# A hybrid attention and state space layer on one core: gate units and the mean square after attention, moved from GpSimd to VectorE

## The chip, the cores and the metric

The kernel runs on one core of one Trainium2 chip. A core has TensorE (PE, matmuls), VectorE (DVE), ScalarE (ACT), GpSimd (POOL) and a queue that only issues transfers (SP); ACT and POOL issue transfers too. Each engine works off its own list of instructions in a fixed order. The metric is device microseconds of one execution, as the median over some runs.

## The reference, cut to what matters

The layer is decoder-like, 1024 positions plus 16 meta tokens, 1024 channels, all in float32:

```python
xn = rmsnorm(h, norm_mix)
q, k, v, u, g_att, g_ssm = jnp.split(xn @ w_in, offs, axis=-1)
attn = sliding_window_attention(q, k, v, sinks)
y = s5_ssm(u, ...)                      # a linear recurrence over the positions
z = jax.nn.gelu(y)
za, zb = jnp.split(z @ w_glu, 2, axis=-1)
ssm = za * jax.nn.sigmoid(zb)
merged = (jax.nn.sigmoid(g_att) * rmsnorm(attn, attn_branch_norm)
          + jax.nn.sigmoid(g_ssm) * rmsnorm(ssm, ssm_branch_norm))
h = h + merged @ w_out                  # then a SwiGLU block
```

What the change touches is the part between attention and `z`: the two gates, the mean square of `attn` that its norm needs, and the product gate x norm x `attn`.

## The kernel before, in words

Activations are held with channels on the 128 partitions and positions along the free side. Each float32 product is made of three passes over a rounded part and a remainder of both operands, so each loaded weight tile `raw` is cast on ACT to `wh` (line 103) and its remainder `wl` is a subtraction (line 104), on POOL unless the caller names another engine. The passes are the matmuls of line 122.

A gate unit (`g_unit`, line 540) is one of 32: unit numbers 0 to 15 make the state space gate (`which` = 1, written to `sg_d`), 16 to 31 the attention gate (`which` = 0). A unit is 8 x 3 matmuls of 128x512, a sigmoid on ACT into a tile `sg` (two buffers), and for `which` = 0 also: a load of attention's output from DRAM into `a` (line 553), its product with the broadcast root `rs_at` (line 554, POOL), a product with the norm's gain and `sg` (line 555, DVE), and a transfer to `pa_d` issued by ACT (line 557). Every second unit loads and splits one weight tile. Units 0 to 6 are put into the attention loop.

After attention the program text has this order. `W`, the state of the recurrence over 130 chunks, is loaded (line 765, 4160 KB). Then attention's output is read back in eight tiles `atf` of 128x1024 (two buffers), squared on ACT and added up in `acc` by seven additions (line 777, POOL). `rstd_cols` makes `rs_at` of it: 8 small matmuls (line 748), a copy of the sum to `ms_at` (line 751, DVE), thirteen tiny instructions on DVE for the reciprocal root (`rsqrt`, lines 151 to 159), matmuls that broadcast it (line 757) and two copies (line 759). Then comes the scan over `W` on DVE: 31 iterations of four instructions that depend on each other (lines 784 to 788), then eight blocks of two `step`s (lines 207 to 213). Then gate units 7 to 31, and then the eight blocks `y` (lines 819, 821: two chains of small matmuls, a Gelu into `z`, transposes `zT`), whose loads `uty`, `tp`, `ct` have three buffers. After them come the products with `w_glu` (`za`, `zb`), with weights split on POOL again.

This order is not the order of execution: a planner sorts the instructions into the engines' lists. It goes by a cost model of its own, takes the instruction whose operands are ready by that model, and among several of them the one that stands first in the text. On the chip the lists are then fixed: an engine whose next instruction waits does nothing else, however much of its list is ready.

Of the kernel before, what the change touches and what calls it, by code (L numbers as in the profile page):

```python
# [8 lines left out]
F32 = mybir.dt.float32  # L9
# [4 lines left out]
ALU = mybir.AluOpType  # L14
# [3 lines left out]
P = 128  # L18
# [16 lines left out]
CK, CV, CU, CGA, CGS = 1024, 1280, 1536, 2560, 3584  # L35
# [11 lines left out]
def hybrid_layer_kernel(ctx: ExitStack, tc: tile.TileContext, x, meta_tokens, norm_mix, w_in, q_norm, k_norm,  # L47
                        attn_sinks, lam_re, lam_im, log_dt, ssm_b_re, ssm_b_im, ssm_c_re, ssm_c_im, ssm_d,
                        w_glu, attn_branch_norm, ssm_branch_norm, w_out, norm_ffn, w_ffn_in, w_ffn_out, out):
    nc = tc.nc  # L50
    x, out = x[0], out[0]
    w_in, w_glu, w_out, w_ffn_in, w_ffn_out = w_in[0], w_glu[0], w_out[0], w_ffn_in[0], w_ffn_out[0]

    def sbuf(name, bufs, side="left"):
        return tc.tile_pool(name=name, bufs=bufs, side=side, reuse_waits="tile")
# [41 lines left out]
    def w_tile(src, shape, name, lo=None, pool=pool_r):  # L97

        raw = pool.tile([P, 1024], F32, tag="raw", name=f"raw_{name}")
        nc.sync.dma_start(out=raw.rearrange("p (a b) -> p a b", a=shape[0]), in_=src)  # L100
        hi = pool_w.tile([P, 1024], F32R, tag="w", name=f"wh_{name}")
        lw = pool_w.tile([P, 1024], F32R, tag="w", name=f"wl_{name}")
        nc.scalar.copy(hi, raw)  # L103
        (lo or nc.gpsimd).tensor_tensor(out=lw, in0=raw, in1=hi.bitcast(F32), op=ALU.subtract)  # L104
        return tuple(t.rearrange("p (a b) -> p a b", a=shape[0]) for t in (hi, lw))

    def w_cols(w, c0, n, name, lo=None, pools=(pool_r,)):

        per = 1024 // n
        parts = []  # L110
        for i in range(KB // per):
            src = w[i * per * P:(i + 1) * per * P, c0:c0 + n].rearrange("(a p) n -> p a n", p=P)
            parts.append(w_tile(src, (per, n), f"{name}_{i}", lo, pools[i % len(pools)]))
        return lambda kb, part: parts[kb // per][part][:, kb % per, :]
# [299 lines left out]
    with sbuf("pp", 1) as pp:  # L414
# [47 lines left out]
        for blk in range(8):  # L462
# [36 lines left out]
            for e in range(2):  # L499
                for j in range(2):  # L500
                    o = bank(f"v{blk}{e}{j}", "q" if j else "x")
                    for k in range(2):
                        g = e + 4 * j + 2 * k
# [26 lines left out]
    def cols_unit(w, h, name):  # L530

        o = bank(name)
        off = OFF[h]
        mm3(o, w, lambda kb, part: cur[h][part][:, kb, off:off + 512], KB)
        return o

    cur, OFF = xn, (16, 0)
    g_w = {}

    def g_unit(i, pool, bufs):  # L540

        which, f, h = 1 - i // 16, i // 2 % 8, i % 2
        if h == 0:
            g_w[which, f] = w_cols(w_in, (CGA, CGS)[which] + f * P, P, f"g{which}{f}")
        cols = slice(512 * h, 512 * h + 512)
        o = cols_unit(g_w[which, f], h, f"g{which}_{f}{h}")
        sg = pool.tile([P, 512], F32, tag="sg", bufs=bufs, name=f"sg{which}{f}{h}")
        nc.scalar.activation(out=sg, in_=o, func=AF.Sigmoid)
        if which:
            nc.scalar.dma_start(out=sg_d[f][:, cols], in_=sg)  # L550
            return
        a_ = pool.tile([P, 512], F32, tag="a", name=f"a{f}{h}")
        nc.sync.dma_start(out=a_, in_=at_d[f][:, cols])
        nc.gpsimd.tensor_tensor(out=a_, in0=a_, in1=rs_at[:, cols], op=ALU.mult)
        nc.vector.scalar_tensor_tensor(out=a_, in0=a_, scalar=gates[:, 0, f:f + 1], in1=sg,
                                       op0=ALU.mult, op1=ALU.mult)
        nc.scalar.dma_start(out=pa_d[f][:, cols], in_=a_)

    with sbuf("ag", 1, "right") as ag, sbuf("at", 2) as at:
# [170 lines left out]
        ng = NPRE  # L730
        for i in range(ng):
            g_unit(i, ag, 1)
        stages = ((q_proj, 10), (values, 0), (p_turn, 1), (scores, 4), (q_turn, 6))
        for i in range(-10, 32):
            for f, ahead in stages:
                if 0 <= i + ahead < 32:
                    f(i + ahead)
            if i in GAT:
                g_unit(ng, ag, 1)
                ng += 1  # L740
    kvp_cm.__exit__(None, None, None)

    def rstd_cols(acc, nb, name, pool):


        o = bank(f"ssq_{name}", "x")
        for b in range(nb):
            nc.tensor.matmul(o[:, b:b + 1], acc[:, b * P:(b + 1) * P], ones[:, 0:1].bitcast(F32),
                             start=True, stop=True)
        ms = pool.tile([P, nb], F32, tag=f"ms{nb}", name=f"ms_{name}")  # L750
        nc.vector.tensor_copy(ms, o[:, 0:nb])
        r = rsqrt(ms, P, nb, pool, name)
        rs = pool.tile([P, nb * P], F32, tag=f"rsb{nb}", name=f"rsb_{name}")
        for h in range(0, nb, 4):
            o = bank(f"rsb_{name}{h}", "x")
            for b in range(4):
                nc.tensor.matmul(o[:, b * P:(b + 1) * P], r[:, h + b:h + b + 1].to_broadcast([P, P]), ident,
                                 start=True, stop=True)
            nc.scalar.copy(rs[:, h * P:(h + 4) * P], o)
        return rs  # L760
# [3 lines left out]
    W = sp.tile([P, 2, GRP // 2, NCH], F32, name="W")  # L764
    nc.sync.dma_start(out=W, in_=v_d)
    gp = scan.enter_context(sbuf("gp", 2))
    with sbuf("vp", 2) as vp:

        acc = vp.tile([P, D], F32, tag="acc", bufs=1, name="acc_at")
        for f in range(KB):  # L770
            a_ = vp.tile([P, D], F32, tag="atf", name=f"atf{f}")
            nc.sync.dma_start(out=a_, in_=at_d[f])
            if f == 0:
                nc.scalar.activation(out=acc, in_=a_, func=AF.Square)
            else:
                nc.scalar.activation(out=a_, in_=a_, func=AF.Square)
                nc.gpsimd.tensor_tensor(out=acc, in0=acc, in1=a_, op=ALU.add)
        rs_at = rstd_cols(acc, 8, "at", sp)


# [1 line left out]
    for c in range(5, NCH - 1, 4):  # L782
        s1 = W[:, :, :, c]
        nc.vector.tensor_tensor(out=m, in0=W[:, :, :, c - 4].unsqueeze(1).to_broadcast([P, 2, 2, GRP // 2]),
                                in1=a32.rearrange("p (k r) g -> p k r g", k=2), op=ALU.mult)
# [7 lines left out]

    yp_cm = sbuf("yp", 2)
    yp = yp_cm.__enter__()
    for i in range(ng, 32):
        g_unit(i, gp, 2)


    zt = new_a("zt")  # L800
    for blk in range(8):
# [13 lines left out]
        for hh in range(2):  # L815
            o = bank(f"y{blk}{hh}")
            for k in range(4):
                g = 4 * hh + k
# [5 lines left out]
                out=z[:, :, 64 * hh:64 * hh + 64].rearrange("p t (g c) -> p g t c", c=16),  # L824
# [20 lines left out]
    with sbuf("mp", 2) as mp:  # L845
        ssm, acc = {}, {}
# [75 lines left out]
    with sbuf("op", 2) as op_:  # L922
# [37 lines left out]
        for n in range(2):  # L960
            w = w_cols(w_out, n * 512, 512, f"o{n}", nc.vector)
            cols = slice(512 * n, 512 * n + 512)
# [331 lines left out]
```

## Time and profile before

| | |
|---|---|
| median of 3 runs | 1725.21 us (1721.61 to 1725.79) |
| the profiled execution | 1730.69 us, its span 1728.9 us |
| PE busy | 1594.5 us, 92% of the span |
| DVE busy | 1200.3 us, 69% |
| ACT busy | 696.6 us, 40% |
| POOL busy | 438.4 us, 25% |
| mean granted clock of PE | 0.962 of full speed |

PE is the busiest engine by far, so a microsecond counts where PE stands still or runs at a lower clock. All times in the rows below are microseconds from the start of the span; attention ends at about 549, the first `za` product starts at about 765.

### The profile page before, as it was taken

What the parts mean: (1) busy time and instruction counts of PE and PEld (TensorE: products, weight loads), DVE (VectorE), ACT (ScalarE), POOL (GpSimd) and SP (SyncE); (2) the same over time, 40 slices, a digit from 0 to 9 for tenths busy, and PEclk for the clock granted to TensorE, in tenths of its full rate; (3) what the DMA queues carried; (4) which work ended last, traced back from release to release, by engine and by line L of the source; (5) the groups of instructions that cost most, each with busy time, mean ns of one, the idle gap of its engine ahead of it and who ended that gap; (6) DMA issues with size and microseconds to landing.
All of it is one profiled execution on the core that took longest, in us unless ns stands there. A gap on an engine that the chain in (4) does not pass through costs nothing.

```text
span 1728.9 us, 22182 instructions
## 1 busy us (share of the span) xinstructions
PE 1594.5 (92%) x8002; PEld 1326.6 (77%) x8002; DVE 1200.3 (69%) x2245; ACT 696.6 (40%) x1363; POOL 438.4 (25%) x312
## 2 busy tenths in 40 slices
PE   7999978989989959699998898899999999899999
PEld 5788868778867848588887786688888888678887
DVE  7779886999983899351115668966665666299973
ACT  4424335878974311262222232533333333234330
POOL 0001103334332613402332400111111112256441
PEclk9999989999989979899999899899999999999999
DMA  5264442011013743572221352233323231385432
GB/s 187 61 138 133 133 143 69 13 40 41 20 49 129 237 135 122 162 217 74 73 74 49 117 167 95 91 117 104 109 93 104 92 113 64 147 327 183 145 112 79
DMA packets 175357, 196.92 MB, mean 114 GB/s; under 512 B 12768, under 2 KB 125408, under 8 KB 175120
## 3 DMA queue, kind: packets, MB, share of 16 engines
q1 hardware_dynamic: 166736, 183.94, 33.0%
q10 hardware_dynamic: 8288, 11.01, 2.0%
q8 instruction: 63, 1.03, 0.3%
q0 software_dynamic: 224, 0.56, 0.1%
q14 instruction: 46, 0.38, 0.1%
HBM read 140.62 MB, written 54.85 MB: 113 GB/s over the span
## 4 chain that ended last, share of the span: by engine, by line
PE 50%; DMA 4%; DVE 4%; issue 1%; POOL 1%; ACT 1%; SPq 0%; ACTq 0%; POOLq 0%
PE ch_fg L905 6%; PE ch_fu L905 6%; PE ch L905 5%; PE wo L122 5%; PE za L122 5%; PE zb L122 5%; PE si L905 4%; PE th_fg L905 3%; PE th_fu L905 3%; PE si_fg L905 2%; PE si_fu L905 2%; DMA tp<-kl_d 1%; PE ch_e L905 1%; DMA a<-at_d 1%; DVE ssm L873 1%; DMA rawa<-act_d 1%
## 5 line engine op out<-in xcount | busy, mean ns | idle before, releaser
L122 PE MATMUL g<-xn,wh_g 128*128 128x512 f32 x512 | 165.9, 404 | 1.0 <-DVE av L726 0.7
L905 PE MATMUL ch<-B,A 128*128 128x512 f32 x528 | 125.7, 394 | 13.0 <-ACT B L1226 7.5
L905 PEld LDWEIGHTS ch<-B,A 128*128 128x128 f32 x528 | 99.8, 190 | 36.5 <-ACT B L1226 9.8
L122 PEld LDWEIGHTS g<-xn,wh_g 128*128 128x128 f32 x512 | 98.0, 193 | 24.3 <-DVE av L726 1.0
L122 PE MATMUL q<-wh_q,xn 128*128 128x256 f32 x512 | 105.1, 293 | 4.1 <-ACT qp L620 4.1
L122 PE MATMUL g<-xn,wl_g 128*128 128x512 f32 x256 | 103.0, 402 | 0.0
L909 POOL TENSOR_TENSOR a<-c,c_fg 128x512 f32<-128x512 f32 x10 | 15.8, 1584 | 315.0 <-DVE c L909 211.0
L122 PE MATMUL wo<-wh_o,mt 128*128 128x512 f32 x256 | 84.5, 409 | 9.3 <-DVE h L982 4.9
L905 PE MATMUL si<-B,A 128*128 128x512 f32 x396 | 92.5, 389 | 0.0
L122 PE MATMUL u<-xn,wh_u 128*128 128x272 f32 (+2 forms) x384 | 92.4, 333 | 0.0
L122 PEld LDWEIGHTS q<-wh_q,xn 128*128 128x128 f32 x512 | 84.9, 196 | 5.8 <-ACT qp L620 4.6
L104 POOL TENSOR_TENSOR wl_g<-raw_g,wh_g 128x1024 fp32r<-128x1024 f32 x16 | 43.4, 2715 | 178.5 <-ACT wh_g L103 172.7
L905 PEld LDWEIGHTS si<-B,A 128*128 128x128 f32 x396 | 74.3, 188 | 15.4
L856 DVE TENSOR_TENSOR ssm<-za,zs 128x512 f32<-128x512 f32 x16 | 11.0, 691 | 105.4 <-ACT zs L855 105.4
L909 DVE TENSOR_TENSOR A<-rawa,A 128x1536 fp32r<-128x1536 f32 (+1 forms) x28 | 76.6, 2734 | 10.7 <-ACT A L1226 10.7
L122 PE MATMUL zb<-zt,wh_zb 128*128 128x512 f32 x256 | 79.3, 390 | 0.0
L122 PE MATMUL za<-zt,wh_za 128*128 128x512 f32 x256 | 79.1, 390 | 0.0
L1226 ACT CAST A<-rawa 128x1536 fp32r<-128x1536 f32 (+1 forms) x28 | 38.5, 1374 | 96.4 <-issue 47.9
L122 PE MATMUL q<-wl_q,xn 128*128 128x256 f32 x256 | 74.4, 291 | 0.0
L909 POOL TENSOR_TENSOR B<-t,B 128x1536 fp32r<-128x1536 f32 (+1 forms) x16 | 59.4, 3723 | 55.5 <-ACT B L1226 55.5
L669 ACT ACTIVATE pr<-pr,mn 128x272 f32<-128x272 f32 (+1 forms) x128 | 64.9, 508 | 16.9 <-DVE mn L663 14.2
L122 PEld LDWEIGHTS u<-xn,wh_u 128*128 128x128 f32 x384 | 66.6, 198 | 5.6
(425 smaller groups left out, 4311.0 us busy)
## 6 DMA issues: line engine op xcount, KB each, us to landing
rawa<-act_d SPq DMA_DIRECT2D x21, 768.0 KB
raw_fg<-in_w_ffn_in_dram SPq DMA_DIRECT2D x20, 512.0 KB
raw_fu<-in_w_ffn_in_dram SPq DMA_DIRECT2D x20, 512.0 KB
rawb<-in_w_ffn_out_dram SPq DMA_DIRECT2D x6, 1536.0 KB
act_d<-a SPq DMA_DIRECT2D x33, 256.0 KB
raw_g<-in_w_in_dram SPq DMA_DIRECT2D x16, 512.0 KB
act_d<-c_fg SPq DMA_DIRECT2D x30, 256.0 KB
u_d<-uf SPq DMA_DIRECT2D x64, 65.0 KB
```

The lines of the kernel that those rows point to most:

```text
L104: (lo or nc.gpsimd).tensor_tensor(out=lw, in0=raw, in1=hi.bitcast(F32), op=ALU.subtract)
L122: nc.tensor.matmul(o, lhs(kb, a), rhs(kb, b), start=(kb == 0 and i == 0), stop=(kb == n - 1 and i == 2))
L669: nc.scalar.activation(out=pr[:, h, :n], in_=pr[:, h, :n], func=AF.Exp, scale=-1.0, bias=mn[:, h:h + 1], accum_out=den[:, h:h + 1])
L856: nc.vector.tensor_tensor(out=dst, in0=oa, in1=sg, op=ALU.mult)
L873: nc.vector.tensor_tensor(out=src, in0=src, in1=rs, op=ALU.mult)
L905: nc.tensor.matmul(o, lhs(kb, a), rhs(kb, b), start=(first and kb == 0 and i == 0), stop=(kb == n - 1 and i == 2), skip_group_check=not first)
L909: eng.tensor_tensor(out=out, in0=in0, in1=in1, op=op)
L1226: nc.scalar.copy(hi, src)
```

## The change

The remaining state space gate units (7 to 15) stand ahead of the mean square in the text; the weight splits of units 7 to 31, the seven additions of the mean square and the sixteen products with `rs_at` go from POOL to DVE; the tile `a` has four buffers in place of two.

```diff
-    def g_unit(i, pool, bufs):
+    def g_unit(i, pool, bufs, lo=None):
         which, f, h = 1 - i // 16, i // 2 % 8, i % 2
         if h == 0:
-            g_w[which, f] = w_cols(w_in, (CGA, CGS)[which] + f * P, P, f"g{which}{f}")
+            g_w[which, f] = w_cols(w_in, (CGA, CGS)[which] + f * P, P, f"g{which}{f}", lo)
...
-        a_ = pool.tile([P, 512], F32, tag="a", name=f"a{f}{h}")
+        a_ = pool.tile([P, 512], F32, tag="a", bufs=4, name=f"a{f}{h}")
         nc.sync.dma_start(out=a_, in_=at_d[f][:, cols])
-        nc.gpsimd.tensor_tensor(out=a_, in0=a_, in1=rs_at[:, cols], op=ALU.mult)
+        nc.vector.tensor_tensor(out=a_, in0=a_, in1=rs_at[:, cols], op=ALU.mult)
...
     gp = scan.enter_context(sbuf("gp", 2))
+    for i in range(ng, 16):
+        g_unit(i, gp, 2, nc.vector)
     with sbuf("vp", 2) as vp:
...
-                nc.gpsimd.tensor_tensor(out=acc, in0=acc, in1=a_, op=ALU.add)
+                nc.vector.tensor_tensor(out=acc, in0=acc, in1=a_, op=ALU.add)
...
-    for i in range(ng, 32):
-        g_unit(i, gp, 2)
+    for i in range(16, 32):
+        g_unit(i, gp, 2, nc.vector)
```

## Rows read from the trace of the kernel before

**Rows 1.** Busy time by stage, attention's end to the first za product.

```profile
core 0: us, PE busy (x) PEld busy (x) DVE busy (x) ACT busy (x) POOL busy (x), PEclk, DMA share, GB/s
549.30:565.90 16.60, 16.60 (x72) 13.44 (x72) 0.83 (x2) 3.93 (x6) 4.80 (x2) 1.00 0.83 319
565.90:623.30 57.40, 55.33 (x247) 44.80 (x245) 54.14 (x124) 16.48 (x20) 27.00 (x11) 1.00 0.74 230
623.30:645.30 22.00, 3.43 (x16) 3.43 (x17) 21.36 (x51) 3.26 (x5) 3.28 (x2) 0.57 0.23 68
645.30:711.10 65.80, 65.57 (x281) 52.82 (x281) 50.12 (x64) 11.31 (x17) 27.39 (x17) 0.99 0.37 117
711.10:733.00 21.90, 8.74 (x60) 8.09 (x59) 7.43 (x6) 6.04 (x9) 8.39 (x5) 0.75 0.62 193
733.00:765.00 32.00, 29.70 (x247) 29.05 (x248) 20.63 (x40) 21.72 (x42) 0.00 (x0) 0.96 0.92 277
```

**Rows 2.** Waits from 549.3 to 765: total us, times, longest us.

```profile
POOL a L554 <- DMA a<-at_d: 47.2, 10, 9.4
...
PE rsb_at L757 <- DVE rs_i_at L159: 20.6, 1, 20.6
...
DVE m L784 <- DMA W<-v_d: 14.9, 1, 14.9
...
PE zT L829 <- ACT z L823: 7.2, 1, 7.2
...
PE y L819 <- ACT sg L548: 5.9, 2, 4.1
```

**Rows 3.** Timeline of PE: start us, us, what, [idle before <- releaser].

```profile
605.61 1.84 PE L748 MATMUL ssq_at<-ones,acc_at 128*128 128x1 f32 x16
...
641.87 3.78 PE L757 MATMUL rsb_at<-ident,rs_i_at 128*128 128x128 f32 x16 [20.64 <-DVE rs_i_at L159]
...
773.55 1.03 PE L829 MATMUL zT<-ident,z 128*128 128x128 f32 x8
```

**Rows 4.** Timeline of DVE.

```profile
567.11 0.40 DVE L784 TENSOR_TENSOR m<-W,a 128x128 f32<-128x128 f32 x1
...
568.23 0.40 DVE L784 TENSOR_TENSOR m<-W,a 128x128 f32<-128x128 f32 x1
...
608.34 2.31 DVE L786 TENSOR_TENSOR W<-W,m 128x64 f32<-128x64 f32 x1
...
630.12 0.16 DVE L751 COPY ms_at<-ssq_at 128x8 f32<-128x8 f32 x1
...
641.66 0.16 DVE L159 SCALAR_TENSOR_TENSOR rs_i_at<-rs_q_at,rs_i_at 128x8 f32<-128x8 f32 x1
```

**Rows 5.** Timeline of POOL.

```profile
607.93 2.58 POOL L104 TENSOR_TENSOR wl_g<-raw_g,wh_g 128x1024 fp32r<-128x1024 f32 x1 [5.83 <-PE g L122]
...
728.99 2.34 POOL L104 TENSOR_TENSOR wl_zb<-raw_zb,wh_zb 128x1024 fp32r<-128x1024 f32 x1
```

**Rows 6.** The chain that ended last, near the end of the gates.

```profile
722.14 5.48 DMA a<-at_d
...
729.07 2.82 DVE a L555
```

**Rows 7.** Groups, 549.3 to 765: busy us, mean ns | idle before us.

```profile
L555 DVE SCALAR_TENSOR_TENSOR a<-a,gates,sg 128x512 f32<-128x512 f32 x16 | 23.0, 1437 | 29.0 <-POOL a L554 29.0
L104 POOL TENSOR_TENSOR wl_g<-raw_g,wh_g 128x1024 fp32r<-128x1024 f32 x9 | 23.0, 2552 | 59.8 <-ACT wh_g L103 54.0 <-PE g L122 5.8
```

**Rows 8.** Tiles with `a` in the name: duration ns min/median/max, first and last start.

```profile
L207 DVE TENSOR_TENSOR cm<-W,a x32: 593/692/1790, 623.4 to 687.2; 128x256 f32<-128x256 f32 x16, 128x512 f32<-128x512 f32 x16
...
L555 DVE SCALAR_TENSOR_TENSOR a<-a,gates,sg x16: 728/752/2878, 651.4 to 729.1; 128x512 f32<-128x512 f32 x16
```

**Rows 9.** Groups of DVE over the whole trace, for prices.

```profile
L909 DVE TENSOR_TENSOR c_fg<-c_fg,c_fu 128x512 f32<-128x512 f32 x30 | 20.6, 686 | 0.1
...
L104 DVE TENSOR_TENSOR wl_u<-raw_u,wh_u 128x1024 fp32r<-128x1024 f32 x8 | 9.8, 1221 | 9.9 <-ACT wh_u L103 9.8
```

## The prediction

> **What bounds the kernel now.** I read the page's busy row first: PE is busiest by far, so I looked for stretches in which PE stands, in the page's forty slices. The ones near the change lie between attention's end and the first `za` product, and a table of busy time by stage cuts that stretch where PE stops and starts [rows 1]. The reader is to see four things there. From 549.3 to 623.3 PE is full but for 2.1 us: gate units 7 and on. From 623.3 to 645.3 it works 3.43 of 22.0 us. From 645.3 to 711.1 it is full again (65.57 of 65.80): the rest of the gate units. From 711.1 to 733.0, the start of the `y` blocks, it works 8.74 of 21.9 us, and from 733 to 765 it is nearly full, with the transfers at 0.92 of their engines.
>
> The waits name the causes [rows 2]. PE waits 20.6 us, once, for the last link of the reciprocal root on DVE. At the start of `y` it waits 5.9 us for sigmoids and 7.2 us for a Gelu.
>
> Then the timelines, for why these are late. The sum of squares is done on PE at 605.61 + 1.84 = 607.5, but its copy starts on DVE only at 630.12, and the root's last link ends at 641.8 [rows 3, 4]. Between stand the scan's instructions, ahead of it in DVE's list. The scan itself is slow: an iteration undisturbed takes 568.23 - 567.11 = 1.12 us, so 31 take 34.7, but they ran from 565.9 to 623.3, 57.4 us [rows 1, 4]. The missing 22.7 us are seen one by one: the addition at 608.34 took 2.31 us, and POOL's split ran from 607.93 to 610.5 [rows 4, 5]. While POOL reads and writes such tiles, DVE's instruction waits it out. So PE's 20.6 us are nearly all POOL holding up DVE.
>
> The second gap hangs on the loop around `a`: with two buffers a load waits for an earlier transfer out, POOL waits 47.2 us in all for loads, DVE 29.0 us for POOL [rows 2, 7]. On the chain the last load takes 5.48 us from 722.14, and the last product of line 555 ends at 731.9 [rows 6]. ACT stands at the issue behind it, and the Gelu that `zT` needs is next in ACT's list.
>
> **The change part by part.**
>
> *Work moved to DVE.* Nine splits of 128x1024 in this stretch [rows 7], seven additions of the same size, sixteen products of 128x512. DVE's own rows give 1.22 us and 0.69 us [rows 9]: 9 x 1.22 + 7 x 1.22 + 16 x 0.69 = 30.6 us more for DVE. POOL has nothing else there until the `za` splits, so what it took from DVE goes: 22.7 us in the scan and, on line 555, 16 x (1.437 - 0.752) = 11.0 us [rows 7, 8], 33.7 us together. DVE comes out even. I take the added work at nothing on PE's path, because DVE's list has a small hole after each link of a serial chain and the planner fills it. Without that cover the bound is the 30.6 us, of which what stands ahead of the root matters: that is a rival below. Below nothing: the 33.7 us less 30.6, worth at most 3 us.
>
> *The root.* With the scan undisturbed and additions that no longer queue behind POOL's splits, the links reach DVE's list in time. PE's wait goes: 20.6 us. The broadcast then also runs at the upper clock: its 16 records took 3.78 us in a stage with a mean granted clock of 0.57, mostly the lower level of 1.2 GHz, and 8 such records take 1.03 us at 2.4 GHz [rows 1, 3], so 3.78 - 2.06 = 1.7 us. Against it: four buffers let two more loads of 256 KB start beside `W`, which DVE waits for [rows 2]; at 319 GB/s [rows 1] 0.52 MB are 1.6 us. And a split and an addition may stand right ahead of a link, 2 x 1.22 = 2.4 us. Ends: 22.3 gained if neither counts; 7 if the rival below decides. I take 20.6 + 1.7 - 1.6 - 2.4 = 18.3 us, near the upper end, since the stall is nearly as long as the hold-up that goes.
>
> *Units 7 to 15 ahead of the mean square.* They already run there on PE [rows 1], so on PE this is worth 0. On SP their weight loads pass the `atf` loads in rank, but two raw buffers space them out as before. Three of their splits fall into attention, on a DVE that is full there; each costs 1.22 us in place of a hold-up of about 2. I take 0, bounds -3 and +3 us.
>
> *The loop around `a`.* Four buffers take the transfer out of the loop, the product on DVE follows its load at once, and ACT's issue no longer waits. What is late next is the sigmoid, which follows the matmuls. In the stage from 711.1 to 733.0 the 60 records of `y` need at the later stage's pace 60 x 29.70 / 247 = 7.2 us, so 21.9 - 7.2 = 14.7 us can go [rows 1], the lower clock (0.75) included. One price I keep: POOL still splits `za` and `zb`, and at 729.07 line 555 took 2.82 us while such a split ran from 728.99 [rows 5, 6], 2.1 us over its median [rows 8]. One such block just ahead of the Gelu is likely: 14.7 - 2.1 = 12.6 us. Ends: 14.7 and 5.
>
> The Trainium skill (SBUF — State Buffer, "SBUF: two separate sides") says that VectorE with two SBUF inputs and GpSimd take one port pair as an exclusive lock, and that the loser stands for the whole instruction. The 2.31 us at 608.34 agree. It speaks against part of this change: the products moved to DVE at the gates' end now meet POOL's `za` splits too. By it every such split would cost the tail its full length, and the sum would be some 7 us smaller; by the row it is one.
>
> **The sum.** 18.3 + 12.6 = 30.9 us. The profiled execution took 1730.7 us (span 1728.9 and 1.8 around it), so 1699.8. It lay 5.5 us over the median of 1725.2; the same off gives 1694.3, said as 1694. After 765 the order is as before and PE is dense, so the gain passes to the end.
>
> **The rivals.**
>
> *POOL's last splits hold up every pair of units in the tail.* A split per two units, four in the last eight, at 2.34 us each [rows 5]: 14.7 - 9.4 = 5.3 in place of 12.6, so 1702. For it: line 555's maximum of 2.878 us [rows 8]. Against: only what stands ahead of the Gelu is on the path. Chance 0.10.
>
> *DVE is the bound.* The root keeps its place behind the scan, and adds and splits now stand in the same list: 565.9 + 1.6 + 34.7 (scan) + 6.8 (623.3 to 630.1, the steps ahead of the copy) + 7 x 1.22 + 5 x 1.22 (splits up to there) + 11.7 (630.1 to 641.8) = 635.3 [rows 1, 4, 9]. PE got to its wait at 641.87 - 20.64 = 621.2 and would wait 14 us: 6.6 gained there, and 6 at the tail, as late steps push the last products: 12.6 in all, 1713. For it: the copy did stand behind the scan. Against: the text has it ahead, and the sum is ready sooner. Chance 0.14.
>
> *The other side: the root falls behind the steps as well.* If the planner, with one engine for all of it, puts the additions so late that the copy comes after the last step, 623.4 to 687.2 [rows 8] stands ahead of it: 687 - 630 = 57 us, less the 11.0 that line 555 no longer loses, 46. The root comes at 681 and PE waits 60 us, 39 more than now; with 12.6 back at the tail the time is 1752. It decides from a wait of 20.6 + 12.6 = 33 us on. For it: DVE was busy 54.14 of 57.4 us in the scan [rows 1]. Against: the additions stand ahead of the scan in the text. Chance 0.08.
>
> *It moves nothing:* PE comes to `y` earlier and waits for its loads. The transfers are at 0.92 there [rows 1], but eating 31 us at 277 GB/s would take 8.6 MB more. Chance 0.05, at 1725.
>
> **How the numbers follow.** The forecast has 0.60, its own range 1684 (22.3 + 14.7 + 3 gained) to 1704; 0.03 is left for faster ways not named. The range has to take in the first two rivals: 1682 to 1718, which adds the runs' own scatter of 2 us below and some 5 us over 1713 for the bounds of -3 and +3; outside stay 0.13 and the forecast's edges. A change under 0.3% (5 us) can't be told from none. Faster: 0.60 + 0.10 + 0.14 + 0.03 = 0.87; same 0.05; slower 0.08.
>
> **What would show it.** Right: in the profile after, scan iterations of 1.12 us without any over 2 us; the wait of the broadcast for the root under 5 us; no wait of line 555 for POOL, and waits at the start of `y` under 5 us together; the first `za` product near 734 in place of 765. Wrong: the copy of the sum still over 10 us after the small matmuls; a new wait of PE for a split on DVE; or `za` that starts earlier with an unchanged end.

## The result and the profile after

The changed kernel took 1694.25 us (median of four runs, 1692.26 to 1697.95); the kernel before, run beside it, 1724.6 (1721.61 to 1725.79). The ratio is 0.9831, 95% interval 0.9816 to 0.9846: faster by 30 us. The forecast was 1694. The total was right in part by luck: two of its terms were wrong by 5 and 6 us with opposite signs, and that is the matter of what follows.

The profiled execution took 1697.95 us, its span 1696.2, with a mean granted clock of 0.975. Lines from 769 on stand two higher than before (the additions are L779, the scan L786 to L790, `y` L821 and L823, `zT` L831). First the page's busy row:

```profile
PE 1586.7 (94%) x8002; PEld 1318.3 (78%) x8002; DVE 1181.0 (70%) x2280; ACT 695.7 (41%) x1363; POOL 372.4 (22%) x277
```

The same stages as in [rows 1], cut where PE now stops and starts (us, then busy time of PE, PEld, DVE, ACT and POOL, the granted clock, the transfers' share, GB/s):

```profile
546.60:564.10 17.50, 17.50 (x76) 14.18 (x77) 3.28 (x4) 3.93 (x6) 0.00 (x0) 1.00 0.84 323
564.10:611.00 46.90, 46.90 (x212) 38.32 (x211) 43.75 (x149) 17.09 (x21) 0.00 (x0) 1.00 0.74 242
611.00:615.00 4.00, 4.00 (x28) 3.56 (x27) 3.80 (x7) 1.17 (x2) 0.00 (x0) 1.00 1.12 329
615.00:688.00 73.00, 69.22 (x300) 55.92 (x298) 65.15 (x107) 14.09 (x20) 7.32 (x3) 1.00 0.49 156
688.00:698.20 10.20, 8.18 (x57) 8.00 (x57) 6.90 (x11) 4.70 (x7) 2.35 (x1) 0.83 0.50 112
698.20:730.20 32.00, 28.55 (x247) 27.91 (x248) 20.65 (x40) 21.58 (x42) 0.00 (x0) 1.00 1.02 308
sum 183.60, PE 174.36 PEld 147.88 DVE 143.53 ACT 62.57 POOL 9.67; mean PE 29.06 PEld 24.65 DVE 23.92 ACT 10.43 POOL 1.61
```

POOL does nothing in the first three stages, the scan takes 46.9 us in place of 57.4, and PE is full from attention's end to 683.8. The stage in which PE worked 3.43 of 22.0 us has no counterpart. DVE, with 30.6 us more work by the prediction's count, is busy 143.5 us up to the first `za`; before it was 154.5 (the DVE column of [rows 1], summed).

The waits that answer to [rows 2], 546.6 to 765 (total us, times, longest us):

```profile
DVE a L554 <- DMA a<-at_d: 6.5, 4, 2.1
...
PE y L823 <- DVE ss L815: 3.8, 1, 3.8
PE y L821 <- DMA tp<-kl_d: 3.4, 3, 2.1
...
DVE a L555 <- ACT sg L548: 3.1, 2, 2.0
...
PE zT L831 <- ACT z L825: 2.0, 1, 2.0
```

PE's wait for the root (20.6 us) and POOL's for loads (47.2 us) are gone; at the start of `y` PE now waits for something that it did not wait for before, DVE's copies `ss` of the scan's state. PE's timeline, to be set beside [rows 3] (start us, us, what, idle before and its releaser):

```profile
599.78 1.84 PE L748 MATMUL ssq_at<-ones,acc_at 128*128 128x1 f32 x16
...
612.00 1.95 PE L757 MATMUL rsb_at<-ident,rs_i_at 128*128 128x128 f32 x16
...
688.03 0.49 PE L823 MATMUL y<-ct,ss 128*128 128x128 f32 x2 [3.82 <-DVE ss L815]
...
698.17 1.09 PE L831 MATMUL zT<-ident,z 128*128 128x128 f32 x8 [1.98 <-ACT z L825]
```

DVE's, beside [rows 4]:

```profile
564.15 0.40 DVE L786 TENSOR_TENSOR m<-W,a 128x128 f32<-128x128 f32 x1 [3.16 <-DMA W<-v_d]
...
565.27 0.40 DVE L786 TENSOR_TENSOR m<-W,a 128x128 f32<-128x128 f32 x1
...
602.41 0.15 DVE L751 COPY ms_at<-ssq_at 128x8 f32<-128x8 f32 x1
...
607.99 0.15 DVE L159 SCALAR_TENSOR_TENSOR rs_i_at<-rs_q_at,rs_i_at 128x8 f32<-128x8 f32 x1
...
669.41 2.77 DVE L207 TENSOR_TENSOR cm<-W,a 128x512 f32<-128x512 f32 x1
...
681.96 2.69 DVE L207 TENSOR_TENSOR cm<-W,a 128x256 f32<-128x256 f32 x1
```

The copy of the sum starts 0.8 us after the small matmuls end (599.78 + 1.84 = 601.6), where it lay 22.7 us behind them. The root is done at 608.1, 3.9 us before PE comes to the broadcast. Two of the steps' products, at 669.41 and 681.96, take 2.7 us where such a one takes 0.6 to 0.7. POOL's timeline has the reason, a split at the same moment each time, and it has two more of them:

```profile
654.83 2.39 POOL L104 TENSOR_TENSOR wl_za<-raw_za,wh_za 128x1024 fp32r<-128x1024 f32 x1 [125.56 <-ACT wh_za L103]
669.11 2.53 POOL L104 TENSOR_TENSOR wl_zb<-raw_zb,wh_zb 128x1024 fp32r<-128x1024 f32 x1 [11.88 <-ACT wh_zb L103]
681.87 2.39 POOL L104 TENSOR_TENSOR wl_za<-raw_za,wh_za 128x1024 fp32r<-128x1024 f32 x1 [10.23 <-ACT wh_za L103]
694.22 2.35 POOL L104 TENSOR_TENSOR wl_zb<-raw_zb,wh_zb 128x1024 fp32r<-128x1024 f32 x1 [9.96 <-ACT wh_zb L103]
```

In the chain that ended last, the path from about 588 to 688 runs over DVE's scan, steps, products and splits, and in three places over a load into `a`, two of them (at 623.55, 5.84 us, and at 652.82, 2.81 us) behind a transfer out of it. DVE is busy 65.15 of the 73.0 us from 615 to 688. Each of POOL's four splits ran beside an instruction of DVE's that lies on this chain (start us, us):

```profile
655.65 2.12 DVE a L554
...
669.41 2.79 DVE cm L207
...
681.96 2.70 DVE cm L207
...
687.56 0.43 DVE ss L815
688.03 0.49 PE y L823 x2
...
694.67 2.46 DVE a L555
697.52 0.61 ACT z L825
698.17 1.09 PE zT L831 x8
```

Undisturbed these four take 0.69, 0.69, 0.60 and 0.75 us, so they stood for 1.4, 2.1, 2.1 and 1.7 us, 7.3 together: the first three ahead of the copies `ss`, the fourth ahead of the Gelu that `zT` reads.

**The balance between the two executions.** Attention ends at 546.6 in place of 549.3: 2.7 us. From there to the last gate matmul it is 137.2 us (to 683.8) in place of 161.8 (to 711.1): 24.6. From there to the first `za` product, at 729.9 in place of 764.8, it is 46.1 in place of 53.7: 7.6. Together 34.9; the spans differ by 32.7.

### The profile page after: what moved, and what is told of

Its sections match the earlier page's. It is cut to its first block, busy times and chain, and to the rows that moved or that the text cites. A ratio compares the mean times of both kernels' runs of the same rounds, so it can differ in the third digit from the quotient of the medians.

```text
span 1696.2 us, 22168 instructions
## 1 busy us (share of the span) xinstructions
PE 1586.7 (94%) x8002; PEld 1318.3 (78%) x8002; DVE 1181.0 (70%) x2280; ACT 695.7 (41%) x1363; POOL 372.4 (22%) x277
## 4 chain that ended last, share of the span: by engine, by line
PE 59%; DVE 14%; DMA 4%; ACT 3%; issue 3%; SPq 0%; POOL 0%; ACTq 0%; DVEq 0%
PE ch_fg L907 6%; PE ch_fu L907 6%; PE ch L907 6%; PE za L122 5%; PE wo L122 5%; PE zb L122 5%; PE si L907 4%; PE g L122 3%; PE th_fg L907 3%; PE th_fu L907 3%; PE q L122 2%; PE si_fg L907 2%; PE si_fu L907 2%; DVE pr L663 1%; DVE cm L207 1%
## 5 line engine op out<-in xcount | busy, mean ns | idle before, releaser
L122 PEld LDWEIGHTS g<-xn,wh_g 128*128 128x128 f32 x512 | 97.2, 192 | 22.7 <-PE s L661 0.3
L911 DVE TENSOR_TENSOR A<-rawa,A 128x1536 fp32r<-128x1536 f32 (+1 forms) x28 | 65.4, 2334 | 12.5 <-ACT A L1228 12.5
L122 PEld LDWEIGHTS wo<-wh_o,mt 128*128 128x128 f32 x256 | 50.0, 196 | 20.5 <-DVE h L984 5.3
```

The lines of the kernel that those rows point to most:

```text
L122: nc.tensor.matmul(o, lhs(kb, a), rhs(kb, b), start=(kb == 0 and i == 0), stop=(kb == n - 1 and i == 2))
L911: eng.tensor_tensor(out=out, in0=in0, in1=in1, op=op)
```

## The experiments

Each ratio is to runs of the kernel before on the same chip. The medians of the kernel before, run beside three groups of experiments, were 1725.97, 1724.93 and 1727.59, so ratios are compared, not times, where it matters. How far two numbers must stand apart is shown by the first experiment.

**A yardstick: the order undone.** Units 7 to 15 stand behind the scan in the text again, the rest as changed.

```diff
-    for i in range(ng, 16):
-        g_unit(i, gp, 2, nc.vector)
...
-    for i in range(16, 32):
+    for i in range(ng, 32):
         g_unit(i, gp, 2, nc.vector)
```

> The changed kernel with gate units 7 to 15 back behind the scan in the text. Every engine's list has the same instructions in the same order as in the changed kernel, so this part of the change does nothing and the run shows the scatter of the measurement: within 3 us of 1694 us. There is no rival, short of a difference in where tiles lie.

Measured: 1694.78 us (five runs, 1688.52 to 1698.42), ratio 0.9806 [0.9785, 0.9827]. Every engine's list of instructions is the same as in the changed kernel, one by one. So this part of the change does nothing, and the same lists gave 0.9831 once and 0.9806 once. A difference of 4 us between two variants below is therefore not told apart.

**Each part undone by itself.** The additions, the splits, the products and the buffers, each put back while the rest stays.

```diff
-                nc.vector.tensor_tensor(out=acc, in0=acc, in1=a_, op=ALU.add)
+                nc.gpsimd.tensor_tensor(out=acc, in0=acc, in1=a_, op=ALU.add)
```

> The changed kernel with the seven additions of the mean square back on POOL, all else as changed. My theory (POOL's instructions hold DVE's up, and that was the 20.6 us): seven additions of 2.4 us hold the scan up by some 7 x 2.1 = 15 us, and in DVE's list the copy of the sum falls back behind all 31 iterations, so the root ends near 635 and PE waits some 15 us for it again: about 1709 us. Rival (only the place in the list counted, not the hold-up): the root ends near 620, when PE comes to it, no wait: 1694 us.

```diff
-        g_unit(i, gp, 2, nc.vector)
+        g_unit(i, gp, 2)
```

> The changed kernel with the weight splits of gate units 7 to 31 back on POOL. Theory: some five splits in the scan hold DVE up by 2.1 us each in place of 1.22 us of work, 4 us more, about as much as the slack the root now has; later splits do the same to the steps, 4 us more for y's copies: PE waits 0 to 5 us for the root and 4 us more at the start of y, about 1699 us. Rival (POOL's splits were the main hold-up): over 1706 us.

```diff
-        nc.vector.tensor_tensor(out=a_, in0=a_, in1=rs_at[:, cols], op=ALU.mult)
+        nc.gpsimd.tensor_tensor(out=a_, in0=a_, in1=rs_at[:, cols], op=ALU.mult)
```

> The changed kernel with the sixteen products with the broadcast root back on POOL. Theory: the root is as early as in the changed kernel (no wait of PE for it); behind it DVE is held up by some 16 x 1.1 us in place of 16 x 0.6 us of work, so the steps end 8 us later and y waits for its copies 4 to 8 us more: about 1700 us. Rival (DVE is not on the path there): 1694 us.

```diff
-        a_ = pool.tile([P, 512], F32, tag="a", bufs=4, name=f"a{f}{h}")
+        a_ = pool.tile([P, 512], F32, tag="a", name=f"a{f}{h}")
```

> The changed kernel with two buffers for attention's output in place of four. Theory: the root is early, but loads wait for transfers out again; at the gates' end ACT stands behind the last transfers and y starts 5 us later: about 1699 us. Rival (the buffers carried the gain at the start of y, some 12 us): 1706 us. Other rival (with the products on DVE two buffers are enough): 1694 us.

| undone | median us | ratio [95%] |
|---|---|---|
| additions | 1701.32 | 0.9856 [0.9829, 0.9882] |
| splits | 1696.25 | 0.9826 [0.9808, 0.9845] |
| products | 1697.93 | 0.9832 [0.9809, 0.9854] |
| buffers | 1693.5 | 0.9813 [0.9787, 0.9839] |

Only the additions may cost something when they go back, some 7 us by the medians, though even there the interval overlaps that of the changed kernel. In that run's timelines of PE and DVE the mean square is late at two places:

```profile
605.78 2.30 PE L748 MATMUL ssq_at<-ones,acc_at 128*128 128x1 f32 x16 [2.60 <-POOL acc_at L779]
...
629.52 3.78 PE L757 MATMUL rsb_at<-ident,rs_i_at 128*128 128x128 f32 x16 [4.40 <-DVE rs_i_at L159]
```

```profile
619.68 0.18 DVE L751 COPY ms_at<-ssq_at 128x8 f32<-128x8 f32 x1
```

The copy stands behind all 31 iterations in DVE's list there (in the changed kernel behind 25), but the broadcast also stands later in PE's list, behind 497 gate matmuls in place of 466, so PE loses 2.6 + 4.4 us at these two places and not 20. The expected loss was larger. For the splits, the products and the buffers no loss is shown: the expectation for the buffers (1699) missed, and its rival, that the buffers bring nothing, held. The run with the products on POOL lies between its theory (1700) and its rival (1694) and decides nothing.

**Each part alone, on the kernel before.** Additions alone, then splits alone.

```diff
-                nc.gpsimd.tensor_tensor(out=acc, in0=acc, in1=a_, op=ALU.add)
+                nc.vector.tensor_tensor(out=acc, in0=acc, in1=a_, op=ALU.add)
```

> The kernel before with the seven additions on DVE and nothing else. The copy of the sum stands in DVE's list after 26 iterations of the scan, in place of 31 and two steps. Theory: POOL's splits still hold the scan up, five of them by some 2.1 us; the root ends near 623, PE comes to it near 612 and waits 11 us in place of 20.6; attention and the start of y are as before: 1715 us. Rival (the place in the list is what counts): no wait for the root, 1703 us.

```diff
-        g_unit(i, gp, 2)
+        g_unit(i, gp, 2, nc.vector)
```

> The kernel before with the splits of units 7 to 31 on DVE and nothing else. Theory: the copy of the sum stays behind all 31 iterations; seven additions on POOL hold the scan up by 15 us, nine splits on DVE add 11 us; the root ends near 630, PE waits some 10 us for it, the start of y is as before; attention, with three of the splits on DVE, is some 3 us shorter: 1713 us. Rival (the splits were the hold-up): no wait for the root, 1703 us.

Measured: 1715.72 us, ratio 0.9942 [0.9922, 0.9962], and 1715.13, 0.9920 [0.9899, 0.9940]. Both times were as expected. Where PE waits was not quite: with the additions alone, the wait for the root is 3.6 us and not 11, and three waits of gate matmuls for sigmoids, 4.7 us together, stand beside it; with the splits alone it is 5.3 us and not 10, with 3.1 us for an addition on POOL beside it. The waits of PE with the additions alone, 546 to 770:

```profile
PE y L819 <- ACT sg L548: 8.2, 3, 4.7
PE zT L829 <- ACT z L823: 7.4, 1, 7.4
PE g L122 <- ACT sg L548: 4.7, 3, 2.1
PE rsb_at L757 <- DVE rs_i_at L159: 3.6, 1, 3.6
```

With either part alone the waits at the start of `y` stay about as long as in the kernel before (5.9 and 7.2 us, [rows 2]).

**The loop around `a` undone whole:** products on POOL and two buffers.

> The changed kernel with both edits to the loop around attention's output undone: products on POOL and two buffers. Each alone cost 0 to 4 us. Theory (either one keeps the loop from falling behind, both gone it falls behind as before): the root stays early, but the start of y waits for sigmoids and a Gelu some 8 to 13 us again: 1703 us. Rival (the start of y is late before only because the root is late): 1698 us, as with the products alone.

Measured: 1701.05 us, ratio 0.9860 [0.9845, 0.9875], as expected. The waits show the loop back in its place, and no wait for the root:

```profile
POOL a L554 <- DMA a<-at_d: 53.5, 11, 10.3
...
DVE a L555 <- POOL a L554: 14.0, 4, 6.9
...
PE y L821 <- ACT sg L548: 7.6, 3, 3.0
PE zT L831 <- ACT z L825: 7.4, 1, 7.4
```

So the additions and the splits together give 1724.93 - 1701.05 = 23.9 us, about what they give alone (9.2 and 12.5). The loop gives the rest, about 7 us, and either the products on DVE or the four buffers seem to be enough for it: undoing one of the two moved the time by no more than the yardstick. But this division of the gain holds only in this order. The run above with the splits back on POOL has the additions and the loop, and it stands at 0.9826 where the additions alone stand at 0.9942: without the splits the loop gives some 20 us, and the splits then add nothing that is shown. PE's waits from attention's end to the first `za` are 24.5 us in all with the additions alone and 7.8 us with the additions and the loop; why was not followed.

**The hold-up alone: POOL kept busy.** Is it POOL that slows DVE, or the lists' order that the change altered? The changed kernel with sixteen additions of 128x1024 on POOL, into a tile that nobody reads. Only POOL's list differs, by these sixteen.

```diff
     with sbuf("vp", 2) as vp:
+        idle = vp.tile([P, 1024], F32, tag="idle", bufs=1, name="idle")
+        for k in range(16):
+            ...
+            nc.gpsimd.tensor_tensor(out=idle, in0=x0, in1=x1, op=ALU.add)
```

> The changed kernel, and sixteen additions of 128x1024 on POOL more, after attention, from tiles that never change into a tile that nobody reads: every other engine has the same instructions in the same order as in the changed kernel. Theory (POOL's instructions hold DVE's up): they run back to back from about 547 on, some nine of them beside the scan; DVE loses about 9 x 2.1 = 19 us there, the root ends near 627, PE comes to it at 612 and waits about 15 us: about 1709 us. Rival (what counted was the place of the root in DVE's list): no change, 1694 us.

Measured: 1710.97 us, ratio 0.9921 [0.9895, 0.9947]: 17 us slower than the changed kernel, near the expected time. POOL's timeline, then DVE's:

```profile
548.31 42.22 POOL L773 TENSOR_TENSOR idle<-xn,xn 128x1024 f32<-128x1024 f32 x16 [14.65 <-PE o L719]
```

```profile
575.61 2.48 DVE L790 TENSOR_TENSOR m<-W,a 128x128 f32<-128x128 f32 x1
578.12 2.46 DVE L792 TENSOR_TENSOR W<-W,m 128x64 f32<-128x64 f32 x1
580.62 2.43 DVE L793 TENSOR_TENSOR W<-W,m 128x32 f32<-128x32 f32 x1
582.94 0.21 DVE L794 TENSOR_TENSOR W<-W,m 128x32 f32<-128x32 f32 x1
...
590.75 0.39 DVE L790 TENSOR_TENSOR m<-W,a 128x128 f32<-128x128 f32 x1
591.18 0.28 DVE L792 TENSOR_TENSOR W<-W,m 128x64 f32<-128x64 f32 x1
```

As long as POOL works, three of the four instructions of an iteration take about 2.45 us each. Three iterations took from 568.46 to 590.75, 22.3 us, where undisturbed ones take 3 x 1.12 = 3.4. At 590.5 POOL ends, and the next instructions take 0.39 and 0.28 us. The consequence on PE came at other places than the broadcast, in PE's timeline:

```profile
598.02 1.22 PE L122 MATMUL g<-xn,wh_g 128*128 128x512 f32 x2 [7.84 <-ACT sg L548]
...
618.97 3.57 PE L748 MATMUL ssq_at<-ones,acc_at 128*128 128x1 f32 x16 [4.13 <-DVE acc_at L783]
```

ACT's timeline has the way from DVE to the first of these waits:

```profile
596.42 1.06 ACT L782 ACTIVATE atf<-atf 128x1024 f32<-128x1024 f32 x1 [15.80 <-DMA atf<-at_d]
```

That load waits for a buffer of `atf`, which an addition gives back, and DVE comes to the addition only behind the held iterations, at 591.74. The sigmoid that PE waits for stands behind this square in ACT's list. PE stood 12.0 us at the two places, and then worked at a mean granted clock of 0.80 (590 to 615) and 0.74 (615 to 635), where it is 1.00 in the changed kernel; so a part of the 17 us is the lower clock behind the stalls. The profiled execution, 1717.52 us, was the slowest of the four, and 4.4 us of its lateness lay ahead of the additions.

This shows the hold-up as a cause by itself, with the lists of the other engines held the same.

**The splits beside the last steps on DVE** (`za` and `zb`, the first two pairs), against the hold-ups from 654 on.

```diff
-            wa = w_cols(w_glu, f * P, P, f"za{f}")
-            wb = w_cols(w_glu, D + f * P, P, f"zb{f}")
+            wa = w_cols(w_glu, f * P, P, f"za{f}", nc.vector if f < 2 else None)
+            wb = w_cols(w_glu, D + f * P, P, f"zb{f}", nc.vector if f < 2 else None)
```

> The changed kernel with the first four weight splits of za and zb on DVE too, so that POOL does nothing between attention and the za products. Theory (two of these splits held DVE's steps up by 2.1 us each, which made PE wait 3.8 us for a copy at the start of y): that wait goes, 1.2 us of work in place of 2.1 us of hold-up for each, and the last product is not blocked: 3 to 5 us less, 1690 us. Rival (DVE is the bound at the gates' end, and has now more to do): 1694 us or more.

Measured: 1694.69 us, ratio 0.9825 [0.9809, 0.9842]: no gain, and PE's wait for the copies is longer, 7.0 us at 690.27 in its timeline:

```profile
690.27 0.79 PE L823 MATMUL y<-ct,ss 128*128 128x128 f32 x2 [7.02 <-DVE ss L815]
```

The rival held: DVE has no room there. What it no longer stands, it now works, and it waits 10.0 us for loads of `a` (546 to 700) where the changed kernel waits 6.5. PE's list also has another order from the first `y` blocks on, so the run does not price the hold-ups by themselves.

**The first copies on ACT**, alone and together with the edit above.

```diff
-                cp_ = nc.vector.tensor_copy if e or ri else nc.scalar.copy
+                cp_ = nc.vector.tensor_copy if (e or ri) and blk > 1 else nc.scalar.copy
```

> The changed kernel with all copies of the scan's state for the first two y blocks on ACT (three of four were on DVE). Theory (behind the root DVE is the bound up to the start of y: with the splits of za off POOL, PE waited 7.0 us for these copies in place of 3.8): PE's wait of 3.8 us goes and DVE has 2.5 us less to do: 2 to 4 us less, 1691 us. Rival (the start of y is bound by the loads of tp and the Gelu as well): 1694 us.

> The changed kernel with the first four weight splits of za and zb on DVE and the copies for the first two y blocks on ACT. Theory (DVE is the bound at the start of y): the four splits cost DVE 4.9 us, the copies give back 2.5 us and take themselves off PE's path: 1691 us, no better than with the copies alone. Rival (POOL's hold-up of the steps was the bound, and the copies hid it): 1687 us.

Measured: 1690.25 us (1688.84 to 1696.58), ratio 0.9785 [0.9762, 0.9807], and 1698.59, 0.9828 [0.9810, 0.9847]. The first is the fastest median of all, but its interval overlaps the yardstick's (not the changed kernel's own), so that it beats the changed kernel isn't shown. In its waits the 3.8 us for DVE's copies have become 2.9 us for ACT's: with the steps themselves late (ACT waits 4.6 us for one), it matters little who copies. The second missed by 7 us; PE waits 7.4 us for ACT's copies there. Its lists are ordered differently, and which part of that costs the time was not settled.

## Why the prediction was right, and where its terms were not

*Work moved to DVE, at nothing on PE's path.* Right up to the root and beyond it, by a wider margin than said. The prediction had 30.6 us added against 33.7 freed, 3 us in all; DVE's busy time up to the first `za` fell by 154.5 - 143.5 = 11.0 us. The hold-ups had cost DVE more than the two groups that were counted show. What failed is the cover. The holes hold tiny instructions: an iteration with three of the root's between its links took 1.12 us (from 603.24), as one without. They do not hold a split or an addition: nine of thirty iterations took 2.1 us or more. The added work cost PE nothing only while DVE was ahead of PE, and not where DVE's list is itself the path, as it mostly is from 588 to 688.

*The root, 18.3 us.* Mis-sized: the stage from attention's end to the last gate matmul gained 24.6. The wait of 20.6 and the broadcast's 3.78 - 1.95 = 1.8 us came as said; the whole stage comes out as 20.9 us less idle time (161.8 - 140.9 busy in [rows 1], none idle after) and 140.9 - 137.2 = 3.7 us less busy time, of which the broadcast is half. Some 0.8 us are the four gate matmuls behind it, which took 1.74 us from 645.30 at a granted clock of 0.83 (645.3 to 650) where four take 0.93; the rest was not followed. The two deductions did not come due. `W`'s first iteration started 17.5 us after attention's end in place of 16.6 (0.9 later and not 1.6), and a split does stand between two links (at 605.86, 1.22 us), but the root was 3.9 us ahead of PE, so neither reached the path. Both were charged as if the root still set PE's time. Of the two causes named, splits and additions on POOL, neither was all of it: alone they gave 12.5 and 9.2 us.

*The order of units 7 to 15, 0 us.* Right, and exactly: the lists are the same without it.

*Three splits in attention, 0 with bounds -3 and +3.* Attention ended 2.7 us earlier. Over the runs here, from the first `wl_g` matmul to attention's last, the eleven traces with the splits on DVE show 338.8 to 344.0 us (mean 340.7) and the three with them on POOL 343.2 to 346.0 (344.6). That speaks for some 4 us and isn't proof, since the two overlap.

*The loop around `a`, 12.6 us.* Mis-sized: 7.6, and the run without it lost 7. The loop's own waits went (POOL's 47.2 and DVE's 29.0 us; DVE now waits 6.5 for loads and 3.1 for sigmoids), though four buffers did not take the transfer out of it altogether: two loads on the chain still stand behind one. But "late next is the sigmoid" was the wrong name. Late next are DVE's copies `ss`, 3.8 us, and then loads of `tp`, 3.4 us, with `zT` still 2.0 behind the Gelu. The waits at the start of `y` are 9.2 us, where under 5 was to be seen. The forecast asked what follows the loop on ACT and not what else `y` reads: with PE's stall gone, DVE no longer has those 20.6 us to work off its steps ahead of `y`. And the price of POOL's splits was one block of 2.1 us; four came, 7.3 us, 5.2 more, which is about the miss. That the miss is this and nothing else is not shown, since the same work on DVE brought no gain. The chain of the kernel before had such blocks in its tail already, beside POOL's splits at 707.42 and 719.28, so the one in [rows 6] was the third and not the only one:

```profile
707.50 2.89 DVE a L555
...
719.35 2.79 DVE a L555
```

*The rivals.* The first came true in its mechanism: each of POOL's four last splits held up an instruction on the chain, for 1.4 to 2.1 us and not the 2.34 it was priced at. The tail's gain of 7.6 us is nearer to its 5.3 than to the forecast's 12.6, and the total was saved by the root. The Trainium skill (SBUF — State Buffer, "SBUF: two separate sides") has the loser of the shared port pair stand for the whole instruction. The two steps' products of 2.7 us agree, and so do the 2.45 us of the scan's instructions beside POOL's additions; the fourth instruction of each iteration, which passed in 0.21 us, is left unexplained. The second rival, DVE as the bound, had the copy behind the scan; it came behind 25 of 31 iterations. With the additions on POOL, or the splits alone on DVE, it does stand behind all 31. Its general claim held in the tail instead, and moving the last splits to DVE as well brought nothing. The third and the fourth did not occur.

*The signs that were named.* Iterations of 1.12 us (564.15 to 565.27), with POOL idle throughout: seen; none over 2 us: not seen, since nine have an addition or a split between their links. The wait for the root under 5 us: there is none. No wait of line 555 for POOL: seen. First `za` near 734: 729.9. Under 5 us of waits at the start of `y`: failed. (The range's lower end is a slip of 1 us: 22.3 + 14.7 + 3 = 40.0 off 1725.2 is 1685, not 1684.)

*What stays open.* Of the 34.9 us at the first `za`, 32.7 were left at the end. With the same lists as the changed kernel, the profiled execution of the yardstick had a span of 1686.7 us, 9.5 less, of which 4.1 lay ahead of the first `za` (725.8) and 5.4 behind it; so 2 us between two executions name no cause.

## What to carry to other kernels

When POOL and DVE share a stretch, price POOL's instruction by what it makes DVE lose, not by POOL's own idle time: a serial chain of small instructions lost a whole POOL instruction at three of its four links. When a stall goes, list everything that the next work reads, and ask for each how long its engine still needs when the stall no longer gives it time. Parts of one change that free the same engine aren't worth what each is when undone: here undoing the splits cost no more than 2 us, and the splits alone gave 12, and the loop was worth 7 us with the splits moved and 20 without.

## What the runs showed of the hardware

Beside back-to-back additions of 128x1024 on POOL, DVE and POOL took turns, nearly one for one: DVE's instructions of 0.22 to 0.40 us ended about 2.5 us apart, except the fourth of each iteration, which passed in 0.21 us. POOL paid nothing for these: its additions started 2.52 us apart beside the scan (575.47 to 583.04) as before it (548.31 to 558.39). Only the two that began beside a split on DVE took longer, 3.50 and 3.30 us, as the duration's maximum shows (ns, min/median/max):

```profile
L773 POOL TENSOR_TENSOR idle<-xn,xn x16: 2428/2446/3495, 548.3 to 588.1; 128x1024 f32<-128x1024 f32 x16
```

In these records the one that came second stood: POOL's addition of 3.50 us began at 558.39, behind DVE's split at 558.35, and DVE's 2.03 us for the first instruction of the scan began at 568.46, behind POOL's addition at 567.87. Moving an operation from POOL to DVE halves it besides: a split of 128x1024 takes 1.22 us on DVE and 2.4 on POOL.
